# Triangular inverses from 16-row blocks, and new durations in the planner that orders the instructions

## Chip, cores and metric

The kernel runs on one core of one Trainium2 chip. Its time is device microseconds (us) of one execution; the figure for the kernel before is the median of three runs, and one more execution was profiled.

## What is computed

The reference is a trunk of 4 layers over 256 latent tokens and 256 context tokens of 1024 channels. Each layer has a token mixer and a dense SwiGLU part (hidden width 2816). In the mixer one input projection (6528 columns) feeds two branches: HGRN2 (4 heads of 128) and RWKV-7 (8 heads of 64, two directions), which are projected, gated and merged. The RWKV recurrence is what matters here:

```python
    def step(S, xt):
        w_t, k_t, b_t, kk_t, v_t = xt[:5]
        sa = -jnp.einsum('...vk,...k->...v', S, kk_t)
        S = S * w_t[..., None, :] + sa[..., None] * b_t[..., None, :] + v_t[..., None] * k_t[..., None, :]
```

The kernel computes it in chunks of 64 tokens. Within a chunk the steps depend on each other through a strictly triangular matrix of 64 by 64, and the kernel needs the inverse of one minus that matrix for each chunk, direction and head. All arithmetic is float32; large products are split in two fp32r halves and made of three matmuls.

## The kernel before

The 512 tokens (256 context, 256 latent) lie along the free axis, channels on the partitions. Each layer (`layer`, L744) first runs the mixer and then the dense stages (the merge of the branches, `w_out`, the two feed-forward products).

The mixer is written as streams (generators): for each of four pairs of heads `rw_pair` (L812) prepares operands, `rw_solve` (L985) makes the inverses, `rw_chain` (L1031) runs the 8 chunks one after another; `hg_head` (L1140) does a head of HGRN2, `gate_tiles` (L1300) the gates. Projections of weights are `proj` (L521), which writes the tile p_ps; the weights are split by ACT (wh) and by DVE in the mixers, by POOL in the dense stages of layers 0 to 2 (wl, `load_split`, L477). The modulation weights are summed on DVE beside other work (`ada_pair`, L658).

`rw_solve(p)` works on 32 matrices at once (2 directions, 8 chunks, 2 heads), kept in ZA (tag AR). The two 32-row diagonal blocks of each are transposed into Lp, a view of LT (tag XS), and inverted by substitution on DVE: 30 steps (L1000), each a product into tmp (tag S) and a sum back into Lp. They are transposed back (L1010), and 64 matmuls of 32 by 32 (L1012 to L1028) make the off-diagonal block, through a tile s_ps and ACT. LT is used half by one solve and half by the next, so a solve waits for the one ahead, and a pair's chain waits for its solve.

No engine's order is written by hand. `Plan` (L93) records every operation as a node with the engines that may run it, a duration (`cost`, L198) and its predecessors. `schedule` (L243) gives each node a rank, the longest path behind it in ns plus a bias by stream (BIAS, L45), and simulates the five engines: the engine that is free first takes the ready node of highest rank, or waits a little for a better one (LOOK, L70). Between engines a hand-over of LAG (L238) ns is counted. TensorE's low clock is simulated with WINDOW and COLD (L73). The order that comes out is emitted, and each engine runs its queue in that order. All engine instructions show the line L343 in the profile, where `emit` issues them, so the rows are told apart by tiles. Matmuls joined by `together` (L140) are one node.

## Time and profile before

| | |
|---|---|
| median of 3 runs | 4348.0 us (4347.94 to 4358.15) |
| profiled execution | 4335.38 us |
| its span, first to last instruction | 4333.6 us |
| mean granted TensorE clock | 0.925 of full speed |
| instructions of PE, DVE, ACT, POOL | 26290, 5759, 4234, 1622 |

The profile is of one execution. Busy time of an engine is the time in which one of its instructions ran; matmul records overlap, so a busy PE is not PE at its peak. One float32 matmul makes two records, one of fp32r operands makes one. The mixers stand at 72 to 658, 1243 to 1800, 2378 to 2930 and 3521 to 4060 us, as their first and last transfers show; the dense stages lie behind each.

### The profile page before, as it was taken

What the parts mean: (1) busy time and instruction counts of PE and PEld (TensorE: products, weight loads), DVE (VectorE), ACT (ScalarE), POOL (GpSimd) and SP (SyncE); (2) the same over time, 40 slices, a digit from 0 to 9 for tenths busy, and PEclk for the clock granted to TensorE, in tenths of its full rate; (3) what the DMA queues carried; (4) which work ended last, traced back from release to release, by engine and by line L of the source; (5) the groups of instructions that cost most, each with busy time, mean ns of one, the idle gap of its engine ahead of it and who ended that gap; (6) DMA issues with size and microseconds to landing.
All of it is one profiled execution on the core that took longest, in us unless ns stands there. A gap on an engine that the chain in (4) does not pass through costs nothing.

```text
span 4333.6 us, 71689 instructions
## 1 busy us (share of the span) xinstructions
PE 3898.9 (90%) x26290; PEld 3081.4 (71%) x26290; DVE 3248.5 (75%) x5759; ACT 2147.8 (50%) x4234; POOL 1901.6 (44%) x1622
## 2 busy tenths in 40 slices
PE   7898898799988988999998889899899987888898
PEld 4666666677776666778777767667777875676898
DVE  5988978977479899675536998987854289888665
ACT  4555653433255556534433556554444254566564
POOL 1343543456533435464553243444555433345332
PEclk8999899999998998999999989889999997798999
DMA  4211137455422111363444111116444331111555
GB/s 149 64 53 46 54 100 219 137 167 157 132 87 62 53 49 51 122 210 100 134 121 136 55 47 55 50 45 216 134 134 129 103 113 43 44 56 52 172 151 161
DMA packets 661409, 451.03 MB, mean 104 GB/s; under 512 B 28224, under 2 KB 584256, under 8 KB 661056
## 3 DMA queue, kind: packets, MB, share of 16 engines
q1 hardware_dynamic: 661056, 446.44, 34.6%
q8 instruction: 207, 3.39, 0.3%
q14 instruction: 146, 1.20, 0.1%
HBM read 416.98 MB, written 29.36 MB: 103 GB/s over the span
## 4 chain that ended last, share of the span: by engine, by line
PE 40%; DVE 18%; issue 3%; ACT 2%; DMA 1%; POOL 1%; DVEq 0%; SPq 0%; POOLq 0%; ACTq 0%
PE p_ps L343 31%; PE s_ps L343 4%; DVE XS L343 3%; PE c_ps L343 3%; PE g_ps L343 2%; DVE wl L343 2%; DVE S L343 2%; DVE AR L343 1%; DVE hX L343 1%; DVE UV L343 1%; DVE X8b L343 1%; DVE X8a L343 1%; DVE fn L343 1%; DVE y L343 1%; DVE og L343 1%
## 5 line engine op out<-in xcount | busy, mean ns | idle before, releaser
L343 PE MATMUL p_ps<-hh,wl 128*128 128x512 f32 (+1 forms) x2784 | 1057.9, 397 | 64.6 <-DVE wl L343 48.7
L343 PE MATMUL p_ps<-hh,wh 128*128 128x512 f32 (+1 forms) x2784 | 1062.5, 393 | 35.7 <-ACT wh L343 24.4
L343 PE MATMUL p_ps<-hl,wh 128*128 128x512 f32 (+1 forms) x2784 | 1055.4, 390 | 0.0
L343 ACT ACTIVATE wh<-wr 128x512 fp32r<-128x512 f32 x986 | 608.4, 621 | 812.7 <-PE p_ps L343 726.6
L343 POOL TENSOR_TENSOR wl<-wr,wh 128x512 fp32r<-128x512 f32 x492 | 673.2, 1371 | 696.5 <-ACT wh L343 501.9
L343 PEld LDWEIGHTS p_ps<-hh,wl 128*128 128x128 f32 x2784 | 539.1, 196 | 198.5 <-DVE wl L343 68.3
L343 PEld LDWEIGHTS p_ps<-hh,wh 128*128 128x128 f32 x2784 | 538.3, 196 | 144.3 <-ACT wh L343 37.0
L343 PEld LDWEIGHTS p_ps<-hl,wh 128*128 128x128 f32 x2784 | 538.9, 196 | 93.1 <-issue 6.2
L343 DVE TENSOR_TENSOR wl<-wr,wh 128x512 fp32r<-128x512 f32 (+1 forms) x494 | 364.8, 743 | 126.0 <-ACT wh L343 80.8
L343 POOL TENSOR_SCALAR fn<-fn 128x512 f32<-128x512 f32 (+1 forms) x152 | 230.9, 1519 | 249.3 <-ACT fn L343 232.2
L343 DVE TENSOR_TENSOR fn<-fn,p_ps 128x512 f32<-128x512 f32 (+1 forms) x208 | 127.4, 615 | 254.8 <-ACT fn L343 152.8
L343 POOL TENSOR_SCALAR S0P<-S,pcs 128x64 f32<-128x64 f32 x192 | 148.4, 791 | 345.1 <-DVE S L343 329.8
L343 ACT ACTIVATE fn<-fn 128x512 f32<-128x512 f32 (+1 forms) x304 | 174.4, 574 | 104.6 <-POOL fn L343 100.3
L343 POOL COPY SC<-XS 64x256 f32<-64x256 f32 x128 | 73.6, 575 | 327.7 <-DVE SC L343 321.9
L343 DVE TENSOR_TENSOR XS<-XS,S 64x30 f32<-64x30 f32 (+14 forms) x480 | 208.2, 434 | 11.3
L343 POOL TENSOR_TENSOR HB<-HB,HA 128x512 f32<-128x512 f32 x112 | 162.6, 1452 | 113.9 <-ACT hY L343 110.6
L343 DVE TENSOR_TENSOR S<-XS 64x30 f32<-64x30 f32 (+14 forms) x480 | 198.7, 414 | 11.1
L343 POOL TENSOR_TENSOR HA<-HA 128x512 f32<-128x512 f32 x112 | 144.4, 1289 | 19.7 <-ACT hX L343 14.0
L343 PE MATMUL p_ps<-SC,wh 128*128 128x512 f32 (+1 forms) x440 | 145.6, 367 | 6.4 <-ACT SC L343 4.3
L343 DVE SCALAR_TENSOR_TENSOR UV<-c_ps,pcs,S0P 64x64 f32<-64x64 f32 x384 | 108.6, 283 | 40.6 <-PE c_ps L343 31.1
L343 ACT ACTIVATE fn<-p_ps 128x512 f32<-128x512 f32 (+1 forms) x217 | 113.1, 521 | 50.9 <-PE p_ps L343 33.8
L343 POOL TENSOR_SCALAR X8a<-X8a 128x512 f32<-128x512 f32 x64 | 106.9, 1670 | 41.2 <-ACT X8a L343 38.7
(477 smaller groups left out, 8781.8 us busy)
## 6 DMA issues: line engine op xcount, KB each, us to landing
wr<-ffn_w SPq DMA_DIRECT2D x512, 256.0 KB, 3.0
wr<-w_in SPq DMA_DIRECT2D x408, 256.0 KB, 2.9
hq<-ada_w SPq DMA_DIRECT2D x242, 256.0 KB, 2.9
PB<-ada_w SPq DMA_DIRECT2D x110, 256.0 KB, 2.9
wr<-w_out SPq DMA_DIRECT2D x64, 256.0 KB, 3.3
gts<-fn SPq DMA_DIRECT2D x48, 256.0 KB, 3.1
wr<-proj_a SPq DMA_DIRECT2D x32, 256.0 KB, 3.7
wr<-proj_b SPq DMA_DIRECT2D x32, 256.0 KB, 4.2
```

The source lines that it names most:

```text
L343: getattr(self.eng[self.on[i]], name)(*args, **kw)
```

## The change

In `rw_solve` the substitution runs over the four 16-row diagonal blocks instead of the two 32-row ones: 14 steps, each for both 16-row blocks of a 32-row block in one instruction (`blocks` is a view over both). The 16 by 16 block between them is then made on TensorE: three transposes (XT, G, XB) prepare operands, two groups of 64 matmuls of 16 by 16 by 16 follow, each with two evictions by ACT. XT and XB lie in LT, G in SX. The memset of the lower left block of Zq[1] goes. The 32 by 32 matmuls behind it are joined in groups of 16.

In the planner, a node of TensorE holds a list of passes, each with its tile shape, place and duration; `run_pe` lets passes in different places of the array overlap, starts one 6 ns after another at the earliest, and books 95 ns (SWITCH) where the shape changes. DVE pays 88 ns (QUAD) where the first partition's group of 32 changes. VectorE and GpSimd instructions that read two tensors or copy hold a shared port (`on_port`). Scans and transposes on DVE get durations of their own, and LAG is shortened in several places. BIAS, LOOK and the streams' start times are as before.

```diff
--- before.py
+++ after.py
@@ -71,6 +71,7 @@
         ('pe', True): 30, ('act', True): 0, ('vec', True): 30, ('pool', True): 0, ('dma', True): 0}
 MAXLOOK = 200
 WINDOW, COLD = 4096 / 1.2, (0.39, 0.87)
+SWITCH, QUAD = 95.0, 88.0
 
 
 def bias_of(bias, kind):
@@ -84,9 +85,8 @@
...
+    def __init__(self, engs, calls, preds, costs, load, kind, port, quad):
+        self.recs, self.port, self.quad = [], port, quad
         self.engs, self.calls, self.preds, self.costs, self.load, self.kind = engs, calls, preds, costs, load, kind
 
 
@@ -185,14 +185,61 @@
             load = b / DMA_RATE if engs[0] == "dma" else 0.0
             if engs[0] == "pe":
                 load = args[1].ap[0][1] / P * (0.37 if out.start_partition() and out.shape[0] <= C else 1.0)
-            self.nodes.append(Node(engs, [(name, args, kw)], preds, costs, load, self.kind))
+            self.nodes.append(Node(engs, [(name, args, kw)], preds, costs, load, self.kind,
+                                   [self.on_port(e, name, out, args, kw) for e in engs],
+                                   out.start_partition() // 32 if "vec" in engs else 0))
         if engs[0] == "pe":
-            x, m = self.nodes[n], 1
-            for s, c in args[1].ap[1:]:
-                m *= c
-            if not join:
-                x.head = 0.0 if name == "transpose" else m / 1.2
-            x.tail = m / 1.2 if m == b // (4 * out.ap[0][1]) and m <= C else 1e9
+            x = self.nodes[n]
+            x.recs += self.passes(name, *args[0:2])
+            if len(x.recs) > 1:
+                x.costs[0] = self.run_pe(x.recs, 0.0, x.recs[0][0], {}, 1)[1]
+
+    @staticmethod
+    def on_port(eng, name, out, args, kw):
+
...
+    @staticmethod
+    def passes(name, out, w):
+
+        k, m, n = w.ap[0][1], 1, 1
+        for s, c in w.ap[1:]:
+            m *= c
+        for s, c in out.ap[1:]:
+            n *= c
+        full = name == "transpose" or w.dtype == F32R
+        mode = tuple(128 if full or x > 64 else 64 if x > 32 else 32 for x in (k, m))
+        at = (0, 0) if full else (w.start_partition(), out.start_partition())
+        if name == "transpose":
+            t = [max(k, 64) / 2.4 + 2.5]
+        elif full:
+            t = [n / 2.4 + (13.0 if n > 256 else 10.0)]
+        else:
+            t = [n / 1.2 + 4.5] * 2
+        return [(mode, at, x, k / P) for x in t]
+
+    @staticmethod
+    def run_pe(recs, t, mode, tiles, slow):
+
+        first = None
+        for md, at, d, _ in recs:
+            if md != mode:
+                t = max([t] + list(tiles.values())) + SWITCH
+                tiles.clear()
+                mode = md
+            t = max(t, tiles.get(at, 0.0))
+            first = t if first is None else first
+            tiles[at] = t + d * slow
+            t += 6.0
+        return first, max(tiles.values()), mode, t
 
     @staticmethod
     def cost(eng, name, out, args, kw):
@@ -223,6 +270,8 @@
         if eng == "vec":
             if name == "memset":
                 return n * 1.05
+            if name in ("transpose", "tensor_tensor_scan"):
+                return n * 1.15 if name == "transpose" else 67.0 + n * 2.08
             two = name in ("tensor_scalar", "tensor_copy") and not psum
             return 67.0 + n * (0.53 if two else 1.042) + 61.0 * ptr
         if name == "memset":
@@ -235,9 +284,9 @@
                                 + (1.66 if kw.get("op1") is not None and "mi" in ops else 0.0))
         return 150.0 + 2.1 * n
 
-    LAG = dict(pe=dict(pe=0.0, act=240.0, vec=240.0, pool=240.0, dma=300.0),
-               act=dict(pe=230.0, act=145.0, vec=143.0, pool=170.0, dma=200.0),
-               vec=dict(pe=245.0, act=130.0, vec=127.0, pool=130.0, dma=200.0),
+    LAG = dict(pe=dict(pe=0.0, act=210.0, vec=210.0, pool=300.0, dma=300.0),
+               act=dict(pe=155.0, act=145.0, vec=143.0, pool=170.0, dma=200.0),
+               vec=dict(pe=135.0, act=130.0, vec=127.0, pool=130.0, dma=200.0),
                pool=dict(pe=205.0, act=72.0, vec=156.0, pool=97.0, dma=200.0))
 
     def schedule(self):
@@ -267,7 +316,8 @@
         on = [None] * N
         bus = 0.0
         edge, busy, cold = WINDOW, 0.0, True
-        tail = 1e9
+        mode, tiles, over = None, {}, []
+        quad, held, holds = 0, 0.0, 0.0
 
         def release(i):
             for e in nodes[i].engs:
@@ -309,18 +359,30 @@
             on[i] = e
             c = x.costs[x.engs.index(e)]
             if e == "pe":
-                if t <= free[e]:
-                    c += max(0.0, x.head - tail)
-                tail = x.tail
...
+                first, end, mode, t1 = self.run_pe(x.recs, t, mode, tiles, 2 if cold else 1)
+                k = max(z[3] for z in x.recs)
+                busy += max(0.0, min(end, edge) - first) * k
+                if end > edge:
+                    over.append((first, end, k))
+                free[e] = t1
+            else:
+                if e == "vec":
+                    t += QUAD * (quad != x.quad)
+                    quad = x.quad
+                on_port = x.port[x.engs.index(e)]
+                if on_port and e == "vec":
+                    t = max(t, held)
+                    holds = t + c
+                elif on_port:
+                    c += max(0.0, 0.5 * (holds - t))
+                    held = t + c
+                end = t + c
+                free[e] = end
             order.append((t, i))
             if e == "dma":
                 bus = max(bus, t) + x.load
@@ -994,35 +1056,71 @@
             Lp = LT[o:o + C].rearrange("p (c j) -> p c j", j=32)
             T1 = LT[z:z + 32].rearrange("p (n c) -> p n c", c=32)
             Hs = LT[z + 32:z + C].rearrange("p (n c) -> p n c", c=32)
+            XT = LT[z:z + C, 0:512].rearrange("p (n c) -> p n c", c=16)
+            XB = LT[z:z + C, 512:1024].rearrange("p (n c) -> p n c", c=16)
+            G = SX[z:z + C, 512:1024]
             tmp = SX[o:o + C, 512:768]
+
+            def blocks(r, nr, c, nc_):
+
+                t = LT[o:o + C, 0:1]
+                return bass.AP(t.tensor, t.offset + 32 * r + c, [t.ap[0], [528, 2], [32, nr], [1, nc_]])
+
             for q in range(2):
                 vec.transpose(Lp[32 * q:32 * q + 32], Zq[q][:, :, 32 * q:32 * q + 32].rearrange("p n i -> p i n"))
-            for i in range(30, 0, -1):
-                n = 31 - i
-                tv = tmp[:, 0:n * i].rearrange("p (c j) -> p c j", j=i)
-                vec.tensor_tensor(out=tv, in0=Lp[:, i + 1:32, i:i + 1].to_broadcast([C, n, i]),
-                                  in1=Lp[:, i:i + 1, 0:i].to_broadcast([C, n, i]), op=ALU.mult)
-                vec.tensor_tensor(out=Lp[:, i + 1:32, 0:i], in0=Lp[:, i + 1:32, 0:i], in1=tv, op=ALU.add)
+            for i in range(14, 0, -1):
+                n = 15 - i
+                tv = tmp[:, 0:2 * n * i].rearrange("p (b c j) -> p b c j", b=2, j=i)
+                vec.tensor_tensor(out=tv, in0=blocks(i + 1, n, i, 1).to_broadcast([C, 2, n, i]),
+                                  in1=blocks(i, 1, 0, i).to_broadcast([C, 2, n, i]), op=ALU.mult)
+                vec.tensor_tensor(out=blocks(i + 1, n, 0, i), in0=blocks(i + 1, n, 0, i), in1=tv, op=ALU.add)
                 yield 1
...
-            vec.memset(Zq[1][:, :, 0:32], 0.0)
+            low = Lp[:, :, 0:16].rearrange("p i j -> p j i")
+            vec.transpose(XT.rearrange("p n j -> p j n"), low)
+            vec.transpose(G.rearrange("p (n j) -> p j n", j=16), low[:, :, ::-1])
+            vec.transpose(XB.rearrange("p n c -> p c n"), Lp[:, 16:32, ::-1])
             for q in range(2):
                 vec.transpose(Zq[q][:, :, 32 * q:32 * q + 32].rearrange("p n c -> p c n"), Lp[32 * q:32 * q + 32])
+            qs = [slice(z + 32 * q, z + 32 * q + 16) for q in range(2)]
+            rows = [slice(32 * q, 32 * q + 16) for q in range(2)]
+            ps = sps()
+            with plan.together(0.55):
+                for n in range(32):
+                    for q in range(2):
+                        pe.matmul(ps[qs[q], n * 16:n * 16 + 16], G[rows[q], n * 16:n * 16 + 16], XB[rows[q], n, :],
+                                  start=True, stop=True)
+            for q in range(2):
+                act.activation(G[rows[q]], ps[qs[q]], AF.Copy)
+            yield 1.5
+            ps = sps()
+            with plan.together(0.55):
+                for n in range(32):
+                    for q in range(2):
+                        pe.matmul(ps[qs[q], n * 16:n * 16 + 16], XT[rows[q], n, :], G[rows[q], n * 16:n * 16 + 16],
+                                  start=True, stop=True)
+            for q in range(2):
+                act.activation(Zq[q][0:16, :, 32 * q + 16:32 * q + 32],
+                               ps[qs[q]].rearrange("p (n c) -> p n c", c=16), AF.Copy)
+            yield 1.5
...
             for hf in range(2):
                 ps = sps()
-                for i in range(16):
-                    n = hf * 16 + i
-                    pe.matmul(ps[z:z + 32, i * 32:(i + 1) * 32], Hs[:, n, :], Zq[1][:, n, 32:C], start=True, stop=True)
+                with plan.together():
+                    for i in range(16):
+                        n = hf * 16 + i
+                        pe.matmul(ps[z:z + 32, i * 32:(i + 1) * 32], Hs[:, n, :], Zq[1][:, n, 32:C], start=True,
+                                  stop=True)
                 act.activation(Zq[0][:, hf * 16:hf * 16 + 16, 32:C],
                                ps[z:z + 32].rearrange("p (a c) -> p a c", a=16), AF.Copy)
                 yield 1.5
```

## Rows read from the trace of the kernel before

**Rows 1.** The page, part 1: busy us, share of the span, instructions of each engine.
```profile
PE 3898.9 (90%) x26290; PEld 3081.4 (71%) x26290; DVE 3248.5 (75%) x5759; ACT 2147.8 (50%) x4234; POOL 1901.6 (44%) x1622
```

**Rows 2.** Windows by stage: mixer, dense, mixer, dense, and so on; first line names columns.
```profile
core 0: us, PE busy (x) PEld busy (x) DVE busy (x) ACT busy (x) POOL busy (x), PEclk, DMA share, GB/s
72.00:658.00 586.00, 532.34 (x4331) 395.90 (x4330) 509.40 (x973) 341.13 (x680) 247.13 (x231) 0.92 0.22 65
658.00:1243.00 585.00, 518.83 (x2412) 409.38 (x2411) 428.38 (x577) 208.52 (x377) 295.14 (x207) 0.96 0.53 156
1243.00:1800.00 557.00, 497.10 (x4094) 376.98 (x4092) 488.82 (x938) 325.35 (x651) 226.29 (x218) 0.91 0.19 56
1800.00:2378.00 578.00, 545.30 (x2678) 438.56 (x2673) 333.58 (x495) 229.23 (x419) 299.10 (x218) 0.98 0.48 143
2378.00:2930.00 552.00, 494.13 (x3977) 375.21 (x3976) 482.93 (x919) 318.04 (x634) 218.12 (x213) 0.89 0.18 53
2930.00:3521.00 591.00, 558.19 (x2772) 447.50 (x2770) 344.02 (x515) 237.08 (x439) 305.90 (x227) 0.97 0.48 143
3521.00:4060.00 539.00, 462.78 (x3913) 372.94 (x3911) 464.27 (x955) 314.85 (x682) 220.64 (x228) 0.85 0.21 64
4060.00:4333.00 273.00, 246.91 (x1942) 239.27 (x1942) 168.32 (x286) 148.35 (x300) 88.75 (x75) 0.95 0.56 162
```

**Rows 3.** Groups by shape, PE, second mixer (1243 to 1800 us): busy, mean ns, idle.
```profile
L343 PE MATMUL p_ps<-hh,wl 128*128 128x512 f32 x334 | 141.0, 433 | 14.5 <-DVE wl L343 14.3
```

**Rows 4.** The chain that ended last: start us, us, what.
```profile
1984.97 81.76 PE p_ps L343 x375
```

**Rows 5.** Timeline of PE, end of the last solve of the second mixer: start us, us.
```profile
1768.09 2.30 PE L343 MATMUL s_ps<-XS,AR 32*32 32x32 f32 x64 [0.57 <-DVE y L343]
1771.79 3.62 PE L343 MATMUL s_ps<-AR,XS 32*32 32x32 f32 x64
1778.20 0.69 PE L343 MATMUL c_ps<-S,AR 64*64 64x64 f32 x8
```

**Rows 6.** Groups by line, DVE, whole span: busy us, mean ns, idle before.
```profile
L343 DVE TENSOR_TENSOR XS<-XS,S 64x30 f32<-64x30 f32 (+14 forms) x480 | 208.2, 434 | 11.3
L343 DVE TENSOR_TENSOR S<-XS 64x30 f32<-64x30 f32 (+14 forms) x480 | 198.7, 414 | 11.1
L343 DVE STREAM_TRANSPOSE XS<-AR 32x1024 f32<-32x1024 f32 x48 | 81.4, 1696 | 8.5 <-PE s_ps L343 7.5
L343 DVE STREAM_TRANSPOSE AR<-XS 32x1024 f32<-32x1024 f32 x32 | 63.6, 1986 | 1.0
L343 DVE TENSOR_TENSOR_SCAN X4c<-rmk,X8a 128x512 f32<-128x512 bf16 x32 | 41.9, 1309 | 4.0 <-ACT X8a L343 3.9
L343 DVE MEMSET AR<- 32x1024 f32 x16 | 14.6, 912 | 4.3 <-issue 4.0 <-PE c_ps L343 0.3
```

**Rows 7.** Groups by shape, DVE, whole span: some shapes of the 15 per instruction.
```profile
L343 DVE TENSOR_TENSOR S<-XS 64x30 f32<-64x30 f32 x32 | 6.5, 202 | 0.6
L343 DVE TENSOR_TENSOR S<-XS 64x84 f32<-64x84 f32 x32 | 9.1, 284 | 0.8
L343 DVE TENSOR_TENSOR S<-XS 64x108 f32<-64x108 f32 x32 | 12.0, 376 | 0.8
L343 DVE TENSOR_TENSOR XS<-XS,S 64x108 f32<-64x108 f32 x32 | 15.4, 480 | 0.7
L343 DVE TENSOR_TENSOR S<-XS 64x130 f32<-64x130 f32 x32 | 14.2, 444 | 0.7
```

**Rows 8.** Timeline of DVE, inside a solve: start us, us.
```profile
1680.66 0.17 DVE L343 TENSOR_TENSOR XS<-XS,S 64x30 f32<-64x30 f32 x1
1680.76 0.68 DVE L343 TENSOR_TENSOR X8a<-X8a 128x512 f32<-128x512 f32 x1
```

**Rows 9.** Timeline of DVE, end of a solve's DVE part: start us, us.
```profile
1467.48 1.24 DVE L343 STREAM_TRANSPOSE XS<-AR 32x1024 f32<-32x1024 f32 x1
```

**Rows 10.** Groups by shape, ACT, whole span.
```profile
L343 ACT ACTIVATE XS<-s_ps 32x512 f32<-32x512 f32 x32 | 18.5, 588 | 42.3 <-PE s_ps L343 42.3
```

More of the change, by code (lines that the diff above doesn't have):

```diff
@@ L84 @@
 class Node:
-    head = tail = 0.0
-    def __init__(self, engs, calls, preds, costs, load, kind):
+    def __init__(self, engs, calls, preds, costs, load, kind, port, quad):
+        self.recs, self.port, self.quad = [], port, quad
         self.engs, self.calls, self.preds, self.costs, self.load, self.kind = engs, calls, preds, costs, load, kind
@@ L191, in add @@
-            for s, c in args[1].ap[1:]:
-                m *= c
-            if not join:
-                x.head = 0.0 if name == "transpose" else m / 1.2
-            x.tail = m / 1.2 if m == b // (4 * out.ap[0][1]) and m <= C else 1e9
+            x = self.nodes[n]
[4 more added lines that the diff above has]
+    def on_port(eng, name, out, args, kw):
+        if eng not in ("vec", "pool"):
+            return False
+        if eng == "pool":
+            return name in ("tensor_tensor", "tensor_copy")
+        ins = [x for x in (kw.get(k) for k in ("in_", "in0", "in1", "data0", "data1", "data")) if hasattr(x, "space")]
+        ins = ins or [x for x in args[1:] if hasattr(x, "space")]
+        if name != "transpose" and any(str(x.space).endswith("PSUM") for x in [out] + ins):
+            return False
+        return len(ins) > 1 or name in ("tensor_scalar", "tensor_copy", "transpose")
@@ L311, in schedule @@
             if e == "pe":
-                if t <= free[e]:
-                    c += max(0.0, x.head - tail)
-                tail = x.tail
                 while t >= edge:
                     cold = busy < (COLD[1] if cold else COLD[0]) * WINDOW
-                    busy = max(0.0, free[e] - edge) if free[e] > edge else 0.0
+                    busy = sum(max(0.0, min(b, edge + WINDOW) - max(a, edge)) * k for a, b, k in over)
+                    over = [z for z in over if z[1] > edge + WINDOW]
                     edge += WINDOW
-                if cold:
-                    c *= 2.0
-                busy += (min(t + c, edge) - t) * x.load
-            end = t + c
-            free[e] = end
+                first, end, mode, t1 = self.run_pe(x.recs, t, mode, tiles, 2 if cold else 1)
[17 more added lines that the diff above has]
+                free[e] = end
             order.append((t, i))
@@ L1013, in rw_solve @@
                 ps = sps()
-                for i in range(16):
-                    n = hf * 16 + i
-                    pe.matmul(ps[z + 32:z + C, i * 32:(i + 1) * 32], Zq[0][:, n, 32:C], T1[:, n, :], start=True,
-                              stop=True)
+                with plan.together():
+                    for i in range(16):
+                        n = hf * 16 + i
+                        pe.matmul(ps[z + 32:z + C, i * 32:(i + 1) * 32], Zq[0][:, n, 32:C], T1[:, n, :], start=True,
+                                  stop=True)
                 act.activation(Hs[:, hf * 16:hf * 16 + 16, :],
@@ L1022, in rw_solve @@
                 ps = sps()
-                for i in range(16):
-                    n = hf * 16 + i
-                    pe.matmul(ps[z:z + 32, i * 32:(i + 1) * 32], Hs[:, n, :], Zq[1][:, n, 32:C], start=True, stop=True)
+                with plan.together():
+                    for i in range(16):
+                        n = hf * 16 + i
+                        pe.matmul(ps[z:z + 32, i * 32:(i + 1) * 32], Hs[:, n, :], Zq[1][:, n, 32:C], start=True,
+                                  stop=True)
                 act.activation(Zq[0][:, hf * 16:hf * 16 + 16, 32:C],
```

## Prediction

> **What bounds the kernel now.** I read the page's engine table first, then the windows by stage, then the groups of DVE by line and by shape, then single stretches of the timeline, for the length of one instruction and the distance to the next. The engine table shows PE at 90% and DVE at 75% of the span [rows 1]; the reader should distrust both as averages. The windows split the span into the four mixers and the four dense stages between them [rows 2]. In the dense stages PE is 89 to 94% busy and DVE 58 to 73%. In the four mixers, 2234 us together, DVE is busy 509, 489, 483 and 464 us, 86 to 88%: all its idle time there is 289 us, 72 per mixer. PE shows 86 to 91% in the same windows, but its records overlap. Of the 4094 in the second mixer, 1005 are of the shape of [rows 3] (three such groups), 433 ns long, while in a dense stretch 375 of them took 81.76 us, one every 218 ns [rows 4]. The 1005 need 219 us; the other 3089, at 36 to 86 ns each by the small groups of [rows 5] (2.30 us for 64, 0.69 us for 8), need 111 to 266. So PE has 330 to 485 us of work in a mixer of 557, and DVE 489 that can't be compressed: DVE is the tighter one there, PE the next. The granted clock is 0.85 to 0.92 in the mixers and 0.95 to 0.98 in the dense stages [rows 2].
>
> **Part 1, the solver on DVE.** There are 16 solves (4 pairs, 4 layers). Today each has 30 steps of two instructions, 960 in all, that take 208.2 + 198.7 = 406.9 us [rows 6]. After the change there are 14 steps, each for both 16-row blocks at once: 448 instructions, of 28, 52, 72, 88, 100, 108 and 112 elements, four of each size per solve. By the rows of the nearest shapes, and between them [rows 7], those take 0.21, 0.25, 0.28, 0.32, 0.40, 0.43 and 0.43 us (the means of these rows hold their waits for POOL, as the sum removed does), 9.3 us per solve and 149 in all. That is 258 us less. An instruction's start lies about 0.08 us before the end of the one ahead (0.17 us long at 1680.66, the next starts at 1680.76: [rows 8]), so 512 fewer instructions free 41 us less than their lengths say: 217. The memset of Zq[1], 14.6 us [rows 6], goes too: 232.
>
> Added on DVE are three transposes per solve, each 64 partitions by 512 elements. No row has that shape. The nearest are 32 by 1024, at 1.24 us for the quick form [rows 9] and 1.7 to 2.0 as a mean [rows 6]. If time goes with the elements, half: 0.62 to 1.0; if it doesn't, 2.0. I take 0.95, nearest to the permuted form that the new ones have, which makes 46 us for 48 of them, bounds 30 and 96. **DVE ends up with 232 - 46 = 186 us less, 46 per mixer** (bounds 136 and 202). DVE's remaining work in a mixer is then about 440 us.
>
> **Part 2, the solver on PE and ACT.** Each solve gains two groups of 64 matmuls, 16 by 16 by 16. The 32-column ones have two records per matmul (64 records for 32 matmuls, [rows 5]), so this is 256 records per solve, 1024 per mixer, 4096 in all. With half the columns, half of 36 ns is the low end, 18 us per mixer; 86 ns, the dearest small record, is the high one, 88 us. I take half of 57 ns (3.62 us for 64), since these groups follow DVE waits and may find the low clock, and since two tiles only overlap if their records interleave: 28 ns, 29 us per mixer, 116 us in all. These 64-record groups stand at PE's head, and projections are queued behind them. PE can carry it: 330 to 485 plus 29 still lies under the mixer's length in most of that range, and I count one third of it, 10 us per mixer, as path. ACT gains four evictions per solve, of 16 by 512; the nearest row has 32 by 512 at 588 ns [rows 10], so 2.4 us per solve, 38 us in all. ACT is 58% busy in the mixers [rows 2] and hides them. If it did not, 9 us per mixer would be the price. In the solve's own series two hand-overs PE to ACT to PE appear, about 2 x (2.5 to 3.6 + 1.2) = 7 to 10 us, against 12 to 14 us of DVE work that leaves the same series; what is late next, the chain of that pair, is not later.
>
> By rows alone the added PE work is 116 us. The Trainium skill (TensorEngine Tiling, Instruction Overhead) says a matmul has a cost of about 60 cycles, so that one with a free size of 1 takes as long as one of 60, and warns against shrinking a small dimension further. By that rule, at 1.2 GHz, an estimate of 50 ns for each of 4096 records gives 205 us in place of 116. The 32-column groups at 36 ns each are below it, which speaks against the rule; no row has 16 columns.
>
> **Sum for the mixers.** Should DVE's idle time stay, a mixer shortens by 46 us; with 10 us of PE in the path, by 36 to 37. Four of them: 147, taken as 150 us. The ends are 202 (nothing of PE in the path, cheap transposes) and, with dear transposes and all 29 us in the path, 136 - 116 = 20.
>
> **Part 3, the planner.** The order of every instruction is drawn anew. The priorities (longest path plus BIAS) keep their form; durations and hand-over times change. The old model prices the scan at 0.60 us, where the row has 1.31; the new one 1.13 [rows 6]. It prices a 512-column matmul at 216 ns, where I see 218; the new one 226. It knew no cost for a change of tile shape. A truer clock in the planner puts fewer instructions at the head of an in-order queue before their inputs exist. What it can win is idle time: 289 us of DVE's in the mixers and 66 + 33 + 33 + 26 = 158 us of PE's in the dense stages [rows 2]. A fifth of it would be 90 us; a worse draw may lose as much. Nothing in the model prefers an order that saves changes of shape; it only books them. I take 15 us of gain, bounds a gain of 90 and a loss of 100.
>
> Sum: 4335.4 (the profiled execution) - 150 - 15 = 4170. That execution lies 12.6 us below the median of the runs, 4348.0, so the forecast is 4183.
>
> **Rivals.** (a) *PE takes over in the mixers*: at the top of its range, 485 + 29 us leaves a mixer of 557 little room, so most of DVE's relief turns into waits for p_ps. For it: PE waits are short even now. [...] A gain of 10 us per mixer, 4308. Chance 0.12. (b) *Both parts pay in full*: 202 us and 60 more from the planner, 4335 - 262 + 13 = 4086. For it: the solve stands in series with its pair's chain, and DVE idles little. Chance 0.15. (c) *Slower, by shorter hand-overs in the plan*: the table LAG drops DVE to PE from 245 to 135 ns, ACT to PE from 230 to 155, PE to DVE from 240 to 210. If real ones are longer where queues are full, a dependent instruction reaches the head of its queue too early, and all behind it wait, on DVE above all. It decides when DVE's idle time in a mixer goes from 72 to over 72 + 37 = 109 us. At 130 the mixer is 21 us longer, 84 in all: 4432. Chance 0.12. (d) *The fixed price of a small matmul*: all 4096 new records take 50 ns, 51 us per mixer, and PE is the bound, so they stand in the path and DVE's 46 us are not seen: +205 less the 60 us of waits that vanish, 4493. Chance 0.02; it is what the page's rule would do here. (e) *The blocks save less than counted*: access over two blocks makes each instruction dearer, and transposes cost 2.0 us. DVE's gain halves, 4335 - 70 - 15 + 13 = 4263. It is inside the forecast's own range.
>
> **How the numbers follow.** The forecast (4110 to 4290) has 0.59. A measurement of this kernel can tell about 0.3%, 13 us: faster means below 4335, slower above 4361. Nearly all of the forecast, (a) and (b) are faster, but a draw of the order may eat a gain: I leave 0.05 for no change, 0.14 for slower ((c) and (d)), 0.81 for faster. The range reaches from below (b), 4060, to 4345, where a small gain and a bad draw meet; outside lie (c), (d) and a few hundredths below.
>
> **What would show it.** 448 instead of 960 of the small DVE instructions, with a sum near 150 us; three more transposes per solve near 0.95 us; 4096 more records of 16 columns, near 28 ns apart; DVE's busy time in a mixer near 440 us, its idle time still near 70; mixers near 510 to 550 us, dense stages within 15 us of now. I am wrong if the mixers shorten by less than 20 us each while DVE has the 46 us less (then PE or the order took it), or if the dense stages move by more than the mixers (then the planner decides and not the solver).

## The result, and the profile after

The changed kernel takes 4405.43 us (median of 4 runs, 4401.15 to 4409.99), the kernel before 4353.07 us beside it (4347.94 to 4359.23). The ratio is 1.0127, 95% interval 1.0112 to 1.0142: slower by 52 to 55 us, where 4183 was forecast, and above the end of the range, 4345.

The engine table of the page of the changed kernel, span 4407.7 us (before: [rows 1], span 4333.6):

```profile
PE 3968.1 (90%) x30386; PEld 3131.3 (71%) x30386; DVE 3074.5 (70%) x5247; ACT 2188.6 (50%) x4298; POOL 1895.9 (43%) x1654
```

DVE has 174 us less to do, and the span is 74 us longer. PE is busy for 69 us more, nearly all of the 74. For the stages I cut both traces anew, each mixer ending at its second load of `SC` from `od`, so that like stands beside like. The kernel before, windows by stage, mixer and dense in turn (columns as in [rows 2]):

```profile
72.00:662.00 590.00, 536.34 (x4348) 399.16 (x4347) 511.03 (x976) 341.51 (x681) 248.42 (x232) 0.92 0.22 66
662.00:1244.00 582.00, 515.83 (x2401) 407.07 (x2400) 427.25 (x576) 208.40 (x378) 293.85 (x206) 0.96 0.53 155
1244.00:1846.00 602.00, 542.10 (x4407) 409.23 (x4406) 514.11 (x992) 349.24 (x700) 246.37 (x231) 0.91 0.22 68
1846.00:2378.00 532.00, 499.30 (x2354) 405.36 (x2353) 307.79 (x439) 205.08 (x371) 279.03 (x205) 0.97 0.46 137
2378.00:2988.00 610.00, 552.09 (x4405) 416.62 (x4404) 516.86 (x994) 349.22 (x698) 242.77 (x232) 0.90 0.22 68
2988.00:3521.00 533.00, 500.22 (x2344) 406.09 (x2342) 310.09 (x439) 205.90 (x375) 281.25 (x207) 0.97 0.46 137
3521.00:4060.00 539.00, 462.78 (x3913) 372.94 (x3911) 464.27 (x955) 314.85 (x682) 220.64 (x228) 0.85 0.21 64
4060.00:4333.00 273.00, 246.91 (x1942) 239.27 (x1942) 168.32 (x286) 148.35 (x300) 88.75 (x75) 0.95 0.56 162
```

The changed kernel, the same view:

```profile
72.00:682.00 610.00, 536.10 (x5301) 410.16 (x5300) 442.19 (x847) 344.51 (x687) 216.13 (x225) 0.87 0.19 56
682.00:1260.00 578.00, 536.41 (x2487) 421.67 (x2486) 451.40 (x600) 220.38 (x394) 303.95 (x210) 0.97 0.54 164
1260.00:1877.00 617.00, 544.53 (x5357) 416.51 (x5355) 445.62 (x852) 345.88 (x696) 223.30 (x228) 0.87 0.20 60
1877.00:2413.00 536.00, 511.17 (x2413) 409.40 (x2414) 343.33 (x461) 217.32 (x392) 288.50 (x210) 0.99 0.48 144
2413.00:3032.00 619.00, 545.92 (x5354) 417.09 (x5353) 446.02 (x853) 347.46 (x694) 226.78 (x228) 0.88 0.19 58
3032.00:3584.00 552.00, 522.39 (x2423) 414.40 (x2421) 349.31 (x462) 217.24 (x391) 290.27 (x212) 0.98 0.47 142
3584.00:4113.00 529.00, 474.44 (x4916) 377.63 (x4915) 405.75 (x827) 325.54 (x697) 217.08 (x229) 0.86 0.22 64
4113.00:4407.00 294.00, 255.08 (x1976) 241.98 (x1975) 166.67 (x258) 147.45 (x303) 129.44 (x107) 0.95 0.53 153
```

In the mixers DVE works 266 us less (2006 to 1740 over the four), 442 to 446 us in the first three, where about 440 was forecast. Part of that is luck: 97 of the 266 us is work that now lies in the dense stages (1213 to 1311 us there). Yet the mixers change by +20, +15, +9 and -10 us: the relief is now DVE's idle time, 335 us before and 635 after. PE is busy 2093 us in the four mixers before and 2101 after, with 950 to 1000 records more in each; the granted clock is 0.87 or 0.88 in the first three, where it was 0.90 to 0.92. The dense stages change by -4, +4, +19 and +21 us; PE has 63 us more in them in sum. Counted by their starts in the trace, 253 of the 512-column matmuls that before lay in a mixer now lie in a dense stage, where one holds PE for 239 ns: 60 of those 63 us. The new records took their place in the mixers.

The pieces of the solver, groups by line, DVE, changed kernel (busy us, mean ns, idle before; they answer to [rows 6]):

```profile
L405 DVE STREAM_TRANSPOSE XS<-AR 32x1024 f32<-32x1024 f32 x48 | 81.5, 1697 | 46.5 <-PE s_ps L405 34.5 <-ACT AR L405 11.5
L405 DVE TENSOR_TENSOR S<-XS 64x28 f32<-64x28 f32 (+6 forms) x224 | 67.2, 300 | 5.7
L405 DVE TENSOR_TENSOR XS<-XS,S 64x28 f32<-64x28 f32 (+6 forms) x224 | 62.5, 279 | 5.7
L405 DVE STREAM_TRANSPOSE XS<-XS 64x512 f32<-64x512 f32 x32 | 31.3, 1036 | 0.3
L405 DVE STREAM_TRANSPOSE S<-XS 64x512 f32<-64x512 f32 x16 | 17.7, 1107 | 0.5
```

The substitution takes 129.7 us (149 forecast), the three new transposes 49.0 (46 forecast). And on PE, groups by shape, changed kernel:

```profile
L405 PE MATMUL s_ps<-XS,S 16*16 16x16 f32 x2048 | 29.1, 176 | 4.8 <-DVE AR L405 3.5 <-ACT X8a L405 0.8 <-DVE XS L405 0.5
L405 PE MATMUL s_ps<-S,XS 16*16 16x16 f32 x2048 | 32.4, 179 | 8.3 <-ACT S L405 5.3 <-issue 2.8
```

The 4096 new records (two for each of 2048 matmuls) hold PE for 61.5 us, 15 ns each. Where they stand, timeline of PE, one solve of the changed kernel's second mixer (start us, us):

```profile
1542.43 1.81 PE L405 MATMUL s_ps<-XS,S 16*16 16x16 f32 x128
...
1545.54 1.55 PE L405 MATMUL s_ps<-S,XS 16*16 16x16 f32 x106 [0.40 <-ACT S L405]
...
1550.65 3.46 PE L405 MATMUL s_ps<-XS,AR 32*32 32x32 f32 x61 [1.24 <-DVE XS L405]
...
1554.06 3.44 PE L405 MATMUL s_ps<-AR,XS 32*32 32x32 f32 x61
```

### The profile page after: what moved, and what is told of

The parts are those of the page before. It is cut to its first block, busy times and chain, and to the rows that moved or that the text cites. A ratio compares the mean times of both kernels' runs of the same rounds, so it can differ in the third digit from the quotient of the medians.

```text
span 4407.7 us, 79653 instructions
## 1 busy us (share of the span) xinstructions
PE 3968.1 (90%) x30386; PEld 3131.3 (71%) x30386; DVE 3074.5 (70%) x5247; ACT 2188.6 (50%) x4298; POOL 1895.9 (43%) x1654
## 5 line engine op out<-in xcount | busy, mean ns | idle before, releaser
L405 PE MATMUL p_ps<-hh,wh 128*128 128x512 f32 (+1 forms) x2784 | 1023.2, 399 | 42.6 <-ACT wh L405 35.7
L405 PE MATMUL p_ps<-hh,wl 128*128 128x512 f32 (+1 forms) x2784 | 1004.2, 393 | 40.6 <-DVE wl L405 40.0
L405 POOL TENSOR_TENSOR wl<-wr,wh 128x512 fp32r<-128x512 f32 x522 | 716.7, 1379 | 702.0 <-ACT wh L405 647.5
L405 PE MATMUL p_ps<-hl,wh 128*128 128x512 f32 (+1 forms) x2784 | 999.4, 390 | 0.0
L405 PEld LDWEIGHTS p_ps<-hl,wh 128*128 128x128 f32 x2784 | 529.9, 194 | 99.9 <-issue 9.1
L405 DVE TENSOR_TENSOR wl<-wr,wh 128x512 fp32r<-128x512 f32 x464 | 349.1, 757 | 207.7 <-ACT wh L405 160.4
L405 POOL TENSOR_SCALAR S0P<-S,pcs 128x64 f32<-128x64 f32 x192 | 128.2, 682 | 318.2 <-DVE S L405 288.9
L405 POOL COPY SC<-XS 64x256 f32<-64x256 f32 x128 | 59.2, 463 | 343.3 <-DVE SC L405 338.5
L405 DVE TENSOR_TENSOR hX<-hX,hq 128x512 f32<-128x512 f32 x128 | 118.7, 927 | 47.7 <-ACT hX L405 46.6
L405 DVE SCALAR_TENSOR_TENSOR y<-hq,cvec,y 128x512 f32<-128x512 f32 x110 | 127.0, 1155 | 6.5 <-DMA hq<-ada_w 6.5
L405 PE MATMUL c_ps<-UV,SC 128*64 128x64 f32 x1024 | 99.0, 248 | 35.9 <-DVE S L405 29.7
```

The costliest lines, as they stand in the source:

```text
L405: getattr(self.eng[self.on[i]], name)(*args, **kw)
```

## The experiments

Three theories at first. **PE**: PE's busy time in the mixers is real, so records added to it are paid and DVE's relief is not. **Planner**: the new order costs, through the shorter hand-overs of `LAG`, and the solver itself gains. **Solver series**: the two new steps PE to ACT to PE make each solve late for its chain.

Each run stands against the kernel before on the same chip. Differences in us are between the medians of runs made side by side. Every run but e17 and e18 has a new order of its instructions. One table behind them sums up their traces.

**The two halves alone.** `e1_solver_only` is the changed kernel with `Plan` as before:

```
-SWITCH, QUAD = 95.0, 88.0
...
+    head = tail = 0.0
...
+            if m == n and m <= 64:
+                return (0.9 if out.start_partition() else 1.75) * m
```

> The planner of before, the solver of after. Theory 'planner' (the 174 us that DVE lost are worth what was forecast, and the new order eats them): 4200 to 4290 us, mixers 25 to 45 us shorter than before. Theory 'solver' (DVE was not what held the mixers; the small matmuls take PE time at the low clock, and the new order is neutral): 4380 to 4420, the low clock in a mixer at about 155 us as in the changed kernel, against 100 before.

Measured: 4400.56 us, +59, ratio 1.0136 (1.0114 to 1.0159), as the theory 'solver' had it.

`e2_planner_only` is the changed planner with the old `rw_solve`:

```
-            for i in range(14, 0, -1):
-                n = 15 - i
+            for i in range(30, 0, -1):
+                n = 31 - i
...
-            ps = sps()
-            with plan.together(0.55):
...
```

> The planner of after, the solver of before. Theory 'planner': 4450 to 4550 us, slower than the changed kernel, since the order costs what the solver gains and more. Theory 'solver': 4330 to 4370, as before, with DVE idle 80 to 90 us in a mixer and the low clock at about 100 us.

Measured: 4366.32 us, +25, ratio 1.0062 (1.0040 to 1.0083), again in the range of 'solver'. Both halves lose; the solver alone loses as much as the whole change.

**The solver's two halves.** `e3_no_pe16` is e1 without the matmuls of 16 by 16:

```
-            ps = sps()
-            with plan.together(0.55):
-                for n in range(32):
-                    for q in range(2):
-                        pe.matmul(ps[qs[q], n * 16:n * 16 + 16], G[rows[q], n * 16:n * 16 + 16], XB[rows[q], n, :],
-                                  start=True, stop=True)
-            for q in range(2):
-                act.activation(G[rows[q]], ps[qs[q]], AF.Copy)
...
```

> The solver of after under the planner of before, without its two groups of 16 by 16 matmuls and their four evictions: the off-diagonal 16 by 16 blocks are left out of the inverses. DVE has all of its relief, PE none of its load. Theory 'PE is the bound, DVE's relief is worth nothing': 4320 to 4350 us, as before. Theory 'DVE is the bound and the small matmuls ate the gain': 4180 to 4250.

Measured: 4310.21 us, -34, ratio 0.9911 (0.9885 to 0.9936). Its engine table (span 4316.5):

```profile
PE 3880.3 (90%) x26290; PEld 3084.0 (71%) x26290; DVE 3044.6 (71%) x5281; ACT 2148.3 (50%) x4234; POOL 1853.2 (43%) x1620
```

DVE has 204 us less than in [rows 1] and only 34 us come back, 10 us more than the PE theory allowed and 60 less than the DVE theory asked for. Against e1 the missing groups are worth 93 us. The run also joins the 32 by 32 matmuls in groups of 16, which no run tests alone; by shape these groups hold PE 99.9 us here and 98.6 before, so nothing of the relief is lost there.

`e4_pe16_added` leaves the old solver and adds such groups, whose sums nothing reads:

```
+            for g in range(2):
+                ps = sps()
+                with plan.together(0.55):
+                    for n in range(32):
+                        for q in range(2):
+                            pe.matmul(ps[z + 32 * q:z + 32 * q + 16, n * 16:n * 16 + 16], Zq[q][0:16, n, 32 * q:32 * q + 16],
+                                      Zq[q][0:16, n, 32 * q + 16:32 * q + 32], start=True, stop=True)
```

> The kernel before, with two groups of 64 matmuls of 16 by 16 by 16 added to each solve, whose results nobody reads. Theory 'PE is the bound': 4385 to 4410 us, 45 to 65 us longer, the 58 to 60 us that these records take on PE. Theory 'DVE is the bound': 4340 to 4360, since PE has idle time beside DVE.

Measured: 4423.69 us, +80, ratio 1.0173 (1.0151 to 1.0194). No series is longer here, since nothing waits for these sums: the records, with their new order, cost nearly what e1 and e3 differ by, and 14 us more than the PE theory's range.

**The planner's two halves.** `e5_lag_only` is the kernel before with the new `LAG` (the rows of the diff), `e6_planner_old_lag` is e2 with the old one, `e7_after_old_lag` the changed kernel with the old one:

```
-    LAG = dict(pe=dict(pe=0.0, act=210.0, vec=210.0, pool=300.0, dma=300.0),
+    LAG = dict(pe=dict(pe=0.0, act=240.0, vec=240.0, pool=240.0, dma=300.0),
-               act=dict(pe=155.0, act=145.0, vec=143.0, pool=170.0, dma=200.0),
-               vec=dict(pe=135.0, act=130.0, vec=127.0, pool=130.0, dma=200.0),
+               act=dict(pe=230.0, act=145.0, vec=143.0, pool=170.0, dma=200.0),
+               vec=dict(pe=245.0, act=130.0, vec=127.0, pool=130.0, dma=200.0),
```

> The kernel before with the shorter hand-over times of after alone. If rival (c) of the prediction explains the 25 us that the new planner costs alone: 4360 to 4375 us. If it is another part of the planner: 4335 to 4350.

> The planner of after with the hand-over times of before, solver of before. If the shorter hand-overs cost the 25 us: 4335 to 4350. If another part does: 4360 to 4375.

> The changed kernel with the hand-over times of before. If solver and hand-overs each cost what they cost alone (59 and 37 to 50 us): 4350 to 4380 us. If the shorter hand-overs hurt only beside the old solver: 4395 to 4410.

Measured: e5 4381.16 us, +37, ratio 1.0074 (1.0049 to 1.0100); e6 4317.92 us, -26, ratio 0.9938 (0.9916 to 0.9961), which beats both kernels; e7 4404.57 us, +63, ratio 1.0146 (1.0131 to 1.0161). e5 lies 6 us above and e6 17 us below the range in which the hand-overs cost the 25 us; both have the sign that it asked for. With the old solver the new hand-overs are what the planner loses by. Beside the new solver they don't matter: the old ones give nothing back.

Is it one direction of `LAG` that hurts? From e6, `e8_lag_to_pe` takes only the shorter times into PE (act to pe 155, vec to pe 135), `e9_lag_from_pe` only those out of PE (210, pool 300), and `e10_more_margin` goes the other way:

```
-    LAG = dict(pe=dict(pe=0.0, act=240.0, vec=240.0, pool=240.0, dma=300.0),
-               act=dict(pe=230.0, act=145.0, vec=143.0, pool=170.0, dma=200.0),
-               vec=dict(pe=245.0, act=130.0, vec=127.0, pool=130.0, dma=200.0),
+    LAG = dict(pe=dict(pe=0.0, act=340.0, vec=340.0, pool=340.0, dma=300.0),
+               act=dict(pe=330.0, act=145.0, vec=143.0, pool=170.0, dma=200.0),
+               vec=dict(pe=345.0, act=130.0, vec=127.0, pool=130.0, dma=200.0),
```

> The new planner, the solver of before, hand-overs of before save those into PE: ACT to PE 155 for 230, DVE to PE 135 for 245. If PE's queue is where a dependent instruction that comes early holds up the projections behind it: 4350 to 4375 us, all of the loss. If it is the queues that PE feeds: 4310 to 4325.

> The same, but only the hand-overs out of PE as in after: 210 for 240 to ACT and DVE, 300 to POOL. If the queues that PE feeds carry the loss: 4350 to 4375. If PE's own queue does: 4310 to 4325.

> The new planner, the solver of before, hand-overs into and out of PE 100 ns longer than before. If a longer hand-over in the plan is a margin that pays (an instruction stands at the head of an in-order queue only when its input is surely there): 4290 to 4320 us. If the old figures were right by measure and a margin only delays: 4330 to 4400. If each change of these figures is just another draw of the order: anywhere from 4300 to 4380, without a trend.

Measured: +20 (1.0049, 1.0032 to 1.0066), +33 (1.0073, 1.0058 to 1.0088) and +68 (1.0158, 1.0143 to 1.0174), that is 46, 59 and 94 us above e6. Shorter or longer, each step of 30 to 110 ns away from the old figures loses. e8 and e9 each show the whole loss that its theory reserved for one of them, so their losses don't add up, and e10 lies above all three of its ranges. On PE e10 issues the records of e6 and no other. Its engine table (span 4407.9):

```profile
PE 3950.3 (90%) x26290; PEld 3084.9 (70%) x26290; DVE 3278.6 (74%) x5741; ACT 2155.9 (49%) x4234; POOL 1917.9 (44%) x1640
```

and that of e6 (span 4311.5):

```profile
PE 3856.3 (89%) x26290; PEld 3033.1 (70%) x26290; DVE 3292.4 (76%) x5740; ACT 2151.2 (50%) x4234; POOL 1903.8 (44%) x1641
```

The same 26290 records hold PE 94 us longer, at a granted clock of 0.914 against 0.927 over the span.

**PE against DVE in the kernel before.** `e11_no_pe32` takes the 32 by 32 matmuls out of the solver, `e12_dve_doubled` makes each product of the substitution twice:

```
-                    pe.matmul(ps[z + 32:z + C, i * 32:(i + 1) * 32], Zq[0][:, n, 32:C], T1[:, n, :], start=True,
-                              stop=True)
...
+                for _ in range(2):
+                    vec.tensor_tensor(out=tv, in0=Lp[:, i + 1:32, i:i + 1].to_broadcast([C, n, i]),
+                                      in1=Lp[:, i:i + 1, 0:i].to_broadcast([C, n, i]), op=ALU.mult)
```

> The kernel before without the 32 by 32 matmuls of the solve, their evictions and the transpose T1 ahead of them: the off-diagonal 32 by 32 blocks of the inverses are left out. PE loses 2048 records, 94 us by start-to-start distances, DVE 20 us of transposes. Theory 'PE's occupied time sets the span': 4235 to 4265 us, 75 to 105 less. Theory 'DVE sets it': 4315 to 4335. If the order drawn matters more than either load: anything between 4235 and 4400.

> The kernel before with the product of each substitution step made twice: 480 more DVE instructions, 200 us by their lengths, 160 without the overlaps, all in the solve's own series. Theory 'PE sets the span, DVE's load counts for about a fifth' (34 us were won for 185 us taken away): 4365 to 4385 us. Theory 'DVE sets it': 4480 to 4540.

Measured: e11 4258.64 us, -83, ratio 0.9810 (0.9794 to 0.9826), for 130 us less of PE; e12 4499.62 us, +157, ratio 1.0364 (1.0349 to 1.0379), for 162 us more of DVE. e11 came as the PE theory had it; e12 lies in the range of the theory 'DVE sets it' and went against the PE theory in its plain form: if DVE idles, 162 us more of it should be partly hidden. Two runs asked whether it is DVE's load or the longer series of the solve.

`e13_dve_elsewhere` loads DVE off that series, `e14_series_longer` lengthens the series with ScalarE:

```
+        ada["w"] = ada.get("w", 0) + 1
+        for _ in range(2 if ada["lo"] is vec and ada["w"] % 2 else 1):
+            ada["lo"].tensor_tensor(out=lo, in0=raw, in1=hi.bitcast(F32), op=ALU.subtract)
...
+            for _ in range(8):
+                act.activation(LT[o:o + C], LT[o:o + C], AF.Copy)
```

> The kernel before, with every second subtraction of wl that VectorE makes in the mixers made twice: about 204 more instructions of some 0.70 us each, 140 to 160 us more of VectorE's busy time, off the series of the solve. Doubling the substitution's products cost 157 us for 162 us of VectorE. Theory load (VectorE is as near its bound as TensorE, any added work on it is paid): 130 to 160 us slower. Theory series (the doubled products cost because they lengthen the solve, for which the chain waits): 0 to 40 us slower.

> The kernel before, with eight in-place copies on ScalarE of the chunk's triangle between the substitution and its transposes in each of the 16 solves: about 7.6 us more of series per solve, some 120 us in all, with no work added to VectorE or TensorE. Theory series: 80 to 130 us slower. Theory load: 0 to 25 us slower, as ScalarE is busy for half of the span.

Measured: e13 4444.26 us, +95, ratio 1.0222 (1.0200 to 1.0243), for 110 us more of DVE; e14 4437.75 us, +88, ratio 1.0211 (1.0184 to 1.0238), for 130 us more of ACT and 15 of DVE. e13 lies between its two ranges, e14 in the range of the series. Neither theory alone: both are paid. So a third one had to be met, that any edit loses a lucky order.

**Is it the order?** `e15_redraw_up` and `e16_redraw_down` draw a new order with nothing else changed:

```
+    for _r in LAG.values():
+        for _k in _r:
+            _r[_k] *= 1.02
```

> The kernel before with every hand-over time of the planner multiplied by 1.02: no instruction is added or removed, and no figure is truer or less true than it was; only the ranks differ in the third digit, so the order is drawn anew. Theory draw (the order of before is one lucky draw among many, and whatever disturbs the ranks loses 20 to 70 us): 20 to 70 us slower. Theory figures (the order depends on how well the figures fit, and the other LAG tables were slower because theirs fit less): within 15 us of before.

> As the run with the factor 1.02, with the factor 0.98: a second draw. Theory draw: 20 to 70 us slower, and not by the same amount as the other. Theory figures: within 15 us of before.

Measured: +2 (0.9999, 0.9989 to 1.0010) and -4 (0.9986, 0.9975 to 0.9996), though in e15's program more than half of PE's instructions stand at another place than before. These two new draws cost nothing that matters. They don't show that no order can: the tables of e8 to e10 moved the time by 46 to 94 us with PE's records unchanged.

`e17_dve_same_order` and `e18_pe16_same_order` keep the order of before and put the extra work in as the instructions are issued (in e18 as four portions of 32 matmuls per solve, one ahead of each 32 by 32 group):

```
-                for name, args, kw in self.nodes[i].calls:
+                for name, args, kw in x.calls * (2 if x.twice and self.on[i] == "vec" else 1):
...
+                for name, args, kw in self.nodes[i].first + self.nodes[i].calls:
```

> The work that was added to VectorE off the solve's series (every second of its subtractions of wl in the mixers made twice), but put in when the instructions are issued, after the order is drawn: the order is that of before, and the planner knows nothing of the addition. With a new order it cost 95 us for 110 us of VectorE. Theory load (VectorE is a second bound under TensorE): 80 to 130 us slower. Theory draw (most of the 95 us came with the new order): 10 to 60 us slower.

> Two unread groups of 64 matmuls of 16x16x16 per solve (4096 records, as the change adds), put in when the instructions are issued, ahead of the four 32x32 groups of each solve, in the order of before. With a new order the same number of records cost 80 us, 75 us of TensorE's busy time. Theory TensorE (it is the bound, and what is added on it is paid): 50 to 90 us slower. Theory draw: 0 to 35 us slower, the rest of the 80 us having come with the new order.

Measured: e17 4432.08 us, +92, ratio 1.0205 (1.0187 to 1.0223), for 139 us more of DVE; e18 4406.07 us, +66, ratio 1.0149 (1.0134 to 1.0165). The draw theory falls in both. The new records of e18, then those of e4, groups by shape, PE:

```profile
L344 PE MATMUL s_ps<-AR 16*16 16x16 f32 x4096 | 67.3, 179 | 13.2 <-issue 6.4 <-DVE AR L344 4.3 <-DVE y L344 1.8
L343 PE MATMUL s_ps<-AR 16*16 16x16 f32 x4096 | 60.9, 178 | 24.2 <-issue 18.6 <-DVE AR L343 5.6
```

67.3 us of records, in an unchanged order, for 66 us of time. What PE waits for, the waits by engine and line (us in total, times, longest); the kernel before:

```profile
PE p_ps L343 <- DVE wl L343: 49.9, 40, 5.3
PE c_ps L343 <- DVE S L343: 45.6, 39, 3.9
...
PE p_ps L343 <- ACT wh L343: 29.5, 30, 3.2
```

e17, the same view:

```profile
PE p_ps L345 <- DVE wl L345: 106.0, 94, 5.8
PE c_ps L345 <- DVE S L345: 49.4, 48, 4.8
PE p_ps L345 <- ACT wh L345: 32.3, 31, 4.3
```

and e14:

```profile
PE p_ps L343 <- ACT wh L343: 72.3, 46, 14.5
PE p_ps L343 <- DVE wl L343: 49.9, 44, 5.4
```

DVE has 25% of its time idle, but the halves of the weights reach PE just in time: with the same order, DVE's extra work makes PE wait for `wl` 94 times in place of 40. In e14 the copies hold up `wh`, which ACT makes, in the same way.

**All traces by one sum.** PE's busy time (engine table) plus all its waits (my sum over every row of the waits view) comes within 17 to 19 us of each span:

| profiled run | span | PE busy | PE's waits | of them for DVE |
|---|---|---|---|---|
| before | 4333.6 | 3898.9 | 418 | 264 |
| changed | 4407.7 | 3968.1 | 422 | 218 |
| e1 solver only | 4401.5 | 3946.6 | 437 | 248 |
| e3 without the 16 by 16 groups | 4316.5 | 3880.3 | 420 | 253 |
| e18 records, same order | 4400.0 | 3961.8 | 421 | 260 |
| e4 records, new order | 4422.4 | 3974.4 | 430 | 245 |
| e17 DVE, same order | 4418.8 | 3918.7 | 483 | 327 |
| e13 DVE, new order | 4438.1 | 3922.7 | 498 | 326 |
| e12 products twice | 4495.1 | 3913.5 | 564 | 368 |
| e14 longer series | 4434.8 | 3909.1 | 508 | 262 |
| e11 without the 32 by 32 groups | 4256.5 | 3769.2 | 470 | 287 |
| e6 planner, old `LAG` | 4311.5 | 3856.3 | 437 | 233 |

This is bookkeeping and no proof that PE is the bound: an engine either works or waits, and the same sum for DVE in the kernel before is 3248.5 + 1021.9 = 4270.4. It tells in which part a difference lies. Records added to PE go into its busy time, about one for one (e18: 63 us for 67 of records; e4: 75 for 61; the changed kernel: 69 for 61). Work added to another engine goes for the most part into PE's waits (e12, e13, e14, e17). The 204 us taken from DVE in e3 did not come out of them: DVE's part of PE's waits fell by 11 us, ScalarE's grew by 17, and the 17 us by which this trace is shorter lie in PE's busy time, with the same records. That PE waits 264 us for DVE is a ceiling too, but one above the 186 us forecast, so it would not have ruled the forecast out.

Where the relief went, DVE's own waits show. The pages' groups by line, the kernel before, e3 and the changed kernel (idle time just before the instructions, and what ended most of it, last):

```profile
L343 DVE TENSOR_TENSOR wl<-wr,wh 128x512 fp32r<-128x512 f32 (+1 forms) x494 | 364.8, 743 | 126.0 <-ACT wh L343 80.8
```

```profile
L343 DVE TENSOR_TENSOR wl<-wr,wh 128x512 fp32r<-128x512 f32 (+1 forms) x493 | 358.5, 732 | 191.8 <-ACT wh L343 141.5
```

```profile
L405 DVE TENSOR_TENSOR wl<-wr,wh 128x512 fp32r<-128x512 f32 x464 | 349.1, 757 | 207.7 <-ACT wh L405 160.4
```

Over all rows of the waits view, DVE's waits grow by 196 us from the kernel before to e3 (1022 to 1218), 101 of them for ScalarE and 90 for PE: DVE is done sooner with the solver and then waits for halves `wh` that ScalarE has not made yet, and for sums of PE. ScalarE's idle time before `wh` in e3, by the page, ends for the most part with a product of PE:

```profile
L343 ACT ACTIVATE wh<-wr 128x512 fp32r<-128x512 f32 x986 | 609.4, 621 | 846.0 <-PE p_ps L343 723.9
```

## Why the prediction was wrong, step by step

**What bounds the kernel: the step that failed.** The prediction took the 86 to 91% of PE in the mixers for 330 to 485 us of work out of 557, since records overlap, and called DVE the tighter engine. So it let DVE's relief count in full, on the condition "Should DVE's idle time stay". It did not stay: 335 us became 635 in the four mixers. The busy time counts an overlap once: it is 497 us in that mixer [rows 2], above the top of the range, and in the four mixers it leaves PE 248 us idle of 2341 (first windows above). The distance of 218 ns [rows 4] is that of an undisturbed dense stretch; in the mixers the 3883 projection matmuls (p_ps) of 512 columns hold 1093 us by their starts, 281 ns each, part of it at the lower clock. DVE at 86 to 88% was called tighter than PE at 86 to 91%; shares so close don't tell which engine's relief is worth what, and no wait was looked up to decide it.

**Part 1, the DVE term: right in size, wrong in worth.** 186 us forecast; 174 measured over the span in the changed kernel, 208 in e1. Substitution and transposes are within 13% of their sums. Its worth was forecast as its size; alone it is worth 34 us (e3), and DVE waits for ScalarE and PE in its place.

**Part 2, the PE term.** 28 ns per record forecast, 15 measured, so 61.5 us in place of 116. But the forecast counted a third, 10 us per mixer, as path: 40 us. All of it is: 66 us in an unchanged order (e18), 80 with a new one (e4), 93 between e3 and e1. In e4 the 32 by 32 groups also become dearer (117.0 us by shape, 98.6 before), in e18 as well (113.5), and the granted clock over the span is 0.917 and 0.919 against 0.925. The rule of the Trainium skill (TensorEngine Tiling, Instruction Overhead) was weighed there at 205 us, 50 ns for each of 4096 records. It speaks of matmuls, and 4096 records are 2048 matmuls: 30 ns each as measured, between an estimate by that rule at 2.4 GHz (25 ns) and one at 1.2 GHz (50 ns), so these runs neither confirm nor refute it. The 36 ns held against it are a record's too: 72 ns per matmul. The evictions of 16 by 512 on ACT and the longer series were costed at nothing; the 93 us between e1 and e3 hold them, the 80 and 66 us of e4 and e18 don't, so 13 to 27 us are left for them, if the orders drawn differ by nothing.

**Sum for the mixers.** Forecast -150. Measured -34 (e3) for DVE's relief and +93 (e1 against e3) for the matmuls and what hangs on them: +59 together, which is e1 itself, as the +93 is taken from it.

**Part 3, the planner.** Forecast -15, measured +25 alone, inside its bounds, and next to nothing on top of the solver (+52 against +59). It has two parts of opposite sign: the new model of passes, port and scans with the old hand-overs gains 26 us (e6), the new hand-overs lose 51 (e2 against e6) or 37 by themselves (e5). Why the old `LAG` is good is open: the figures matter (e8 to e10) while two small redraws do not (e15, e16), yet both directions lose.

**The rivals.** (a) had the right mechanism, PE taking over, with the wrong price: it kept a gain of 10 us per mixer. (d) had the mechanism of the loss, records in the path, with 205 us for 61. (c) gave the nearest time, 4432, and its sign was seen: DVE idles 123 to 173 us per mixer, above its 109. But that is DVE's relief and not a late hand-over: with the old hand-overs the changed kernel is no faster (e7). (b) and (e) are out.

**What would show it.** Both signs of error that were named have come: mixers that shorten by less than 20 us while DVE has its relief, and dense stages that move by more than the mixers (+40 and +34 us in sum). But the second does not mean here what it was to mean, that the planner decides: e1 has the old planner and loses 59. Of the +21 us in the last dense stage no run tells the cause: 8 of them are PE's busy time, 13 its idle time, and POOL has 107 instructions there, 75 before.

What stays open: whether the wait of DVE for `wh` and of ScalarE for PE is what keeps DVE's relief at 34 us. The waits of e3 fit it, but no run makes `wh` come sooner, and e3 has a new order of its own, so some tens of its us may belong to the order. PE's wait for the chain, `c_ps` for `S`, grew there too (56.4 us, 45.6 before).

## What to carry to other kernels

Two engines that are both near 90% busy can't be told apart by these shares. Adding work to each can do it, with the order kept (e17, e18). Here, what was added to PE was paid about in full, and what was added to DVE was paid at 0.66 to 0.97 of its size (e17, e13, e12), since it feeds PE just in time; what was taken from DVE returned 0.17 (e3), and DVE then waited for the next engine. So price a relief by what the relieved engine will wait for next, and not by its busy time. Here, work moved from an engine with 25% idle time to one with 10% lost even at a third of the price. And measure both halves of such a change by themselves, one without its cost and one with its cost alone.

## What was not expected of the hardware

A matmul record of 16 columns in two alternating places of the array takes 14 to 16 ns (128 in 1.81 us at 1542.43, granted clock 0.83 from 1542 to 1545 us; 67.3 us for 4096 in e18), against 36 to 57 ns for the 32-column records of [rows 5] (granted clock 0.63 from 1768 to 1776 us). And PE's busy time is no constant of a program: the same 26290 records took 3856.3 us in e6 and 3950.3 in e10, with the order and nothing else on PE different, at granted clocks of 0.927 and 0.914. Nor is a record's length its price: records of the p_ps shape are 433 ns long on average in the second mixer [rows 3], at a granted clock of 0.91, and 391 ns in the stretch of [rows 4], at 1.00, where they start every 218 ns.
